# A two-layer hybrid encoder on one core: zero products ahead, halved first pages, norm rows in place, a held key rotation and another order at the end

## The chip, the cores and the metric

One core of one Trainium2 chip runs the whole program. The metric is the device time of one execution in microseconds (us); less is better. TensorE is called PE here, its weight load PEld, VectorE DVE, ScalarE ACT, GpSimd POOL, SyncE SP. Weights and activations lie in device memory (HBM); the working memory of the core is SBUF, and PE writes its sums to PSUM, of which one bank holds 128x512 numbers of 32 bits.

## The reference

x has 256 rows (tokens) of 4096 numbers. Two layers follow one another, then a last RMS norm:

```
h   = rmsnorm(x, norm_w)
a_q, a_k, a_v, a_g, r_q, r_k, r_v, r_g = split(h @ w_in)      # 4096 x 11264
att = silu(a_g) * attention(rope(rms(a_q)), rope(rms(a_k)), a_v)   # 16 heads, 4 for keys and values
ret = silu(r_g) * ret_norm * rms(retention both ways (r_q, r_k, r_v))  # 8 heads of 256
x   = x + concat(att, ret) @ w_out                            # 4096 x 4096
```

All is float32. `norm_w`, `ret_norm` and `final_norm` are gains by column.

## The kernel before

**Products.** The two projections are nearly all the work. The input projection has 11 blocks in each layer and the output projection 4; a block is two column tiles of 512 for all 256 tokens, so four quarters of 128 tokens by 512 columns. Its 4096 inputs are taken in 16 pairs of k tiles (two times 128 rows). In five pairs (`SEVEN`: 0, 3, 6, 9, 12) the 2x2 block product is made of seven products of sums, as Strassen does; the other eleven take eight, of which two are with the difference of the operands (`x3`). The sums go to seven PSUM banks, M1 to M7, and `combine` (L1266) adds these into the two results `ca` and `cb` when a bank has its last product. Each product is made of three matmuls, since an operand is split into a high part rounded to the matmul's type and a low rest: high by high, weight's low by operand's high, weight's high by operand's low (`product`, L822 to 826).

**Weight pages.** `Weights.load` (L385, DMA at L392 on SP's queue) brings 512 KB pages (`wraw`, five buffers). `parts` (L395) makes the high part `whi` on ACT and the low part `wlo` on DVE, in rings of five buffers, so a page's cast waits until PE has used the page five before it. A pair of `SEVEN` makes two more pages of sums on DVE (`wsum`). In five pairs of each block the second page is "far" (`far_parts`, L411): ACT writes `fhi` and its negative into `flo`, and a DMA of POOL's queue adds the page from HBM onto `flo` (L467), with one buffer each. Where the traces show L198, that is the helper through which every DVE and ACT operation is called.

**Operands.** `split_pair` (L499) turns rows of activations (`full`, 512 KB chunks of two pairs, eight to a stage) into operands: `x7h`, `x7l` for pairs of `SEVEN`; `x8h`, `x8l` and `x3` (`x` in the traces) for others. At a layer's input the gain `nw` is applied here: in place on ACT for pairs of `SEVEN`, and inside the cast and the subtraction for the others. Chunks come back from HBM through POOL's queue, but the last two of a stage are kept in SBUF (`put`, L611), turned by copies on ACT (`move`, L790), and split when `split_late` (L586) is called.

**Order.** The program writes one order for each engine and the engines keep it. A planner does that while it goes through the products: `now.t` counts PE's time by the costs of L43 to 60, a clock for DVE and one for ACT say when these would be done, and after each product `tick` (L744) lets waiting side work (attention, retention, splitting: lanes and tasks that `yield` a delay) go a step further when `Weights.room` (L469) finds that the next pages stay in time; there MARGIN is a reserve, PE_REST is the delay behind a side product, LANDING and FETCH are delays for DMAs, and AT_ONCE bounds the tasks begun. Where PE needs an operand that isn't there, `need` (L599) writes the missing steps at once.

**Places that the change touches.** `keys_values` (L1134) ends the block of keys and values: it loads tables (`plain_tables`, L315, the DMA of the gains at L321) and calls `rotary`, whose first DVE operations, C and S, multiply the tables by the gain. `retention_pair` (L1105) loads 256 KB of `ret_norm` gains on SP and multiplies the gate by them (`gate`, L893). `attention_rest` (L996) loads keys, values and queries (L1001, L787) and stores its result on POOL's queue (L1021). The last block's banks are closed in the order M2, M5, M3, M4 (`last_combine`, L1351); behind M3 and behind M4 `finish` (L1377) squares both tiles of one half of the tokens, sums ten columns of partial sums, takes the power on POOL (L346), and scales and stores eight tiles of 128x512 on SP's queue (L1401). At the start, SP brings the first chunk of x in two halves and the first pages; pair 1 is split first, by hand, then pair 0:

```python
first_rows(0)
weights.load()
...
split_operand(0, 0)
made(1)
begun()
...
begun()
made(0)
```

## Time and profile before

| | us |
|---|---|
| median of 3 runs | 2660.36 (2659.83 to 2660.64) |
| the profiled execution | 2660.69 |
| its span | 2658.5 |
| first matmul of PE starts | 8.95 |
| last matmul of PE starts | 2640.72 |
| mean granted PE clock | 0.993 |

A page of the profile tells for each engine the busy time, its share of the span and the number of instructions; the span is one execution on the chip. Groups of instructions have the line, the engine, the operation and "out<-in" by the program's names. In a timeline the first number is the start and the second the time it took, both in us, for `xN` instructions that follow one another; the bracket at the end tells how long the engine had been idle and what released it. Matmuls overlap: an instruction of 0.39 us may start 0.227 us after the one before. In a table of windows come the stretch, then the busy time and number of instructions of PE, PEld, DVE, ACT and POOL, then the clock granted to PE (1.00 is full), the busy share of the DMA engines and GB/s.

Three groups show how large the page work is:

```profile
L198 DVE TENSOR_TENSOR wlo<-wraw,whi 128x1024 fp32r<-128x1024 f32 (+1 forms) x812 | 894.9, 1120 | 281.4 <-ACT whi L198 275.4
L198 ACT CAST whi<-wraw 128x1024 fp32r<-128x1024 f32 (+1 forms) x812 | 778.8, 971 | 509.4 <-PE M L826 371.8
L467 POOL DMA_DIRECT2D flo<-in_w_in x108 | 97.4, 902 | 1076.1 <-ACT flo L198 1047.9
```

After the bar stand the busy time and the mean ns of one, then the idle time of the engine ahead of them and what ended most of it: ACT's casts wait for PE to free a ring buffer, DVE's low parts wait for the cast.

### The profile page before, as it was taken

The numbers are of one execution on the slowest core, as the hardware profiler recorded it, in microseconds if no ns is written. First come the engines' busy times: TensorE is split into PE (matmuls) and PEld (weight loads), VectorE is DVE, ScalarE is ACT, GpSimd is POOL, SyncE is SP. The second block draws the span as 40 slices with busy tenths as digits, with TensorE's granted clock in tenths as the row PEclk, the third lists the DMA queues.
The fourth block names the chain that finished last, engine by engine and source line by source line (L and its number), as shares of the span: only waits on it lengthen the run. The fifth ranks groups of instructions, "written<-read, shape, count | busy, mean of one in ns | idle before, by whom it ended". The sixth has DMA issues, their size and how long they took to land.

```text
span 2658.5 us, 33938 instructions
## 1 busy us (share of the span) xinstructions
PE 2609.4 (98%) x11742; PEld 2164.3 (81%) x11742; DVE 2153.8 (81%) x2701; ACT 1782.2 (67%) x2518; POOL 365.0 (14%) x508
## 2 busy tenths in 40 slices
PE   7999999999999999999999999999999999999997
PEld 5878888878888888888878888888888888888886
DVE  8878878878878899777989778877888788986775
ACT  6766776766665687665877666766666557876554
POOL 0011211211111010111111112211111111010000
PEclk9999999999999999999999999999999999999998
DMA  7888888888877887988988889889887788778895
GB/s 251 291 244 277 262 276 277 272 256 254 246 233 235 258 260 234 284 259 262 303 255 246 274 282 277 253 254 293 263 271 221 239 258 247 248 239 258 253 279 176
DMA packets 201981, 685.99 MB, mean 258 GB/s; under 512 B 24272, under 2 KB 30928, under 8 KB 201808
## 3 DMA queue, kind: packets, MB, share of 16 engines
q1 hardware_dynamic: 148912, 523.35, 56.4%
q0 software_dynamic: 52896, 160.46, 26.1%
q8 instruction: 92, 1.51, 0.2%
q14 instruction: 81, 0.66, 0.1%
HBM read 639.68 MB, written 44.04 MB: 257 GB/s over the span
## 4 chain that ended last, share of the span: by engine, by line
PE 81%; DVE 8%; DMA 6%; issue 2%; ACT 2%; POOL 1%; SPq 0%; DVEq 0%; POOLq 0%; ACTq 0%
PE M L825 26%; PE M L826 26%; PE M L824 26%; DVE wlo L198 4%; DMA flo<-in_w_in 2%; DMA wraw<-in_w_in 2%; DVE wsum L198 1%; PE ps L825 1%; PE ps L824 1%; PE ps L826 1%; DMA wraw<-in_w_out 1%; ACT whi L198 1%; DMA tables<-in_k_norm 1%; DVE ca L198 0%; DVE cb L198 0%
## 5 line engine op out<-in xcount | busy, mean ns | idle before, releaser
L198 DVE TENSOR_TENSOR wlo<-wraw,whi 128x1024 fp32r<-128x1024 f32 (+1 forms) x812 | 894.9, 1120 | 281.4 <-ACT whi L198 275.4
L198 ACT CAST whi<-wraw 128x1024 fp32r<-128x1024 f32 (+1 forms) x812 | 778.8, 971 | 509.4 <-PE M L826 371.8
L824 PE MATMUL M<-whi,x8h 128*128 128x512 f32 x1536 | 600.8, 391 | 0.5 <-DVE ca L198 0.5
L825 PE MATMUL M<-wlo,x8h 128*128 128x512 f32 x1536 | 600.4, 391 | 0.0
L826 PE MATMUL M<-whi,x8l 128*128 128x512 f32 x1536 | 600.0, 391 | 0.0
L824 PE MATMUL M<-whi,x7h 128*128 128x512 f32 x1050 | 410.0, 390 | 1.5 <-DVE cb L198 1.5
L825 PE MATMUL M<-wlo,x7h 128*128 128x512 f32 x1050 | 409.4, 390 | 1.9 <-DVE wlo L198 1.9
L826 PE MATMUL M<-whi,x7l 128*128 128x512 f32 x1050 | 409.0, 389 | 0.0
L198 DVE TENSOR_TENSOR wlo<-wsum,whi 128x1024 fp32r<-128x1024 f32 x300 | 365.5, 1218 | 24.1 <-ACT whi L198 23.5
L198 ACT CAST whi<-wsum 128x1024 fp32r<-128x1024 f32 x300 | 314.7, 1049 | 101.8 <-PE M L826 87.5
L824 PEld LDWEIGHTS M<-whi,x8h 128*128 128x128 f32 x1536 | 290.1, 189 | 60.8 <-DVE ca L198 0.9
L826 PEld LDWEIGHTS M<-whi,x8l 128*128 128x128 f32 x1536 | 289.9, 189 | 60.8
L825 PEld LDWEIGHTS M<-wlo,x8h 128*128 128x128 f32 x1536 | 290.1, 189 | 59.5
L198 ACT CAST fhi<-wraw 128x1024 fp32r<-128x1024 f32 x148 | 155.7, 1052 | 197.9 <-PE M L826 193.4
L467 POOL DMA_DIRECT2D flo<-in_w_in x108 | 97.4, 902 | 1076.1 <-ACT flo L198 1047.9
L824 PEld LDWEIGHTS M<-whi,x7h 128*128 128x128 f32 x1050 | 197.6, 188 | 43.7 <-DVE cb L198 2.9
L825 PEld LDWEIGHTS M<-wlo,x7h 128*128 128x128 f32 x1050 | 197.6, 188 | 42.3 <-DVE wlo L198 2.2
L826 PEld LDWEIGHTS M<-whi,x7l 128*128 128x128 f32 x1050 | 197.4, 188 | 41.3
L198 DVE TENSOR_TENSOR wsum<-wraw 128x1024 f32<-128x1024 f32 x150 | 182.6, 1218 | 45.0 <-DMA wraw<-in_w_in 39.8
L824 PE MATMUL M<-whi,x 128*128 128x512 f32 x512 | 199.9, 390 | 11.7 <-ACT whi L198 8.9
L825 PE MATMUL M<-wlo,x 128*128 128x512 f32 x512 | 200.4, 391 | 7.5 <-DVE wlo L198 7.5
L826 PE MATMUL M<-whi,x 128*128 128x512 f32 x512 | 200.2, 391 | 3.2 <-DVE x L198 3.2
(219 smaller groups left out, 3390.2 us busy)
## 6 DMA issues: line engine op xcount, KB each, us to landing
wraw<-in_w_in SPq DMA_DIRECT2D x703, 512.0 KB, 5.0
wraw<-in_w_out SPq DMA_DIRECT2D x256, 512.0 KB, 4.9
flo<-in_w_in POOLq DMA_DIRECT2D x108, 512.0 KB, 7.7
flo<-in_w_out POOLq DMA_DIRECT2D x40, 512.0 KB, 7.8
full<-next_dram POOLq DMA_DIRECT2D x18, 512.0 KB, 8.1
p_dram<-room POOLq DMA_DIRECT2D x64, 128.0 KB, 4.6
pT<-p_dram POOLq DMA_DIRECT2D x16, 512.0 KB, 9.8
next_dram<-room POOLq DMA_DIRECT2D x40, 128.0 KB, 5.5
```

The source lines that it names most:

```text
L198: return call(out, *args, **kwargs)
L467: self.adds.pop(0)[1]()
L824: nc.tensor.matmul(out, a[0], b[0], start=start, stop=False)
L825: nc.tensor.matmul(out, a[0], b[1], start=False, stop=False)
L826: nc.tensor.matmul(out, a[1], b[0], start=False, stop=stop)
```

## The change

- **Zeros first.** `warm` sets a small tile to zero and issues 36 matmuls of 128x256 on it (bfloat16, into a PSUM tile that nothing reads), ahead of everything else on PE.
- **First pages in halves.** The very first page is cast and subtracted in two halves of 128x512; the first block's first four products are sorted by half, with the `x3` product behind the other of its half; the first chunk's second half (pair 1) is loaded first, and pair 1's operand, and the first page, are written in an order by hand. The host gives x in plain columns of tokens, so operands of the first stage are cut out of `whole` rows.
- **Norm rows in place.** `ret_norm` joins the table `nw`, and its gains are applied to the rows of the output projection's operands (pairs 8 to 15) instead of the gate; the load of gains, the multiplication and a delay go from `retention_pair`. Gains are applied in place on ACT for all pairs but the very first, and what follows is the cast and subtraction without gains: where before `x8l` took four operations of 128x128 at a stage with gains, it takes one of 128x512 or two of 128x256.
- **Last block.** The order of the banks is M5, M2, M3, M4, and the last products of pair 14 on pages that are still in the ring (M4's) are moved to the end, behind M3's. Squares are taken by bank, one operation on 512 columns each, eight columns of partial sums; output tiles are scaled and stored in a list by hand with an engine named for each.
- **Key rotation.** `keys_values` yields LANDING between the tables' load and the rotation.
- **Planner numbers.** FETCH 14 to 12, FAR_LANDING 12 to 11, MARGIN 0.8 to 0, PE_REST 1.0 to 1.5, AT_ONCE 3 to 2. They enter the order of all side work.

In instructions (rows of the built programs, before to after): PE 11,744 to 11,816 with the loads of weights of the zeros, DVE 2425 to 2411, ACT 1720 to 1756, SP 102 to 82, POOL 282 to 281.

```diff
-STORE, FETCH = 8.0, 14.0
-FAR_LANDING = 12.0
-MARGIN = 0.8
+STORE, FETCH = 8.0, 12.0
+FAR_LANDING = 11.0
+MARGIN = 0.0
 EARLY = 0.7
 NEED = {"ak": 4, "ag": 3, "rk": 4, "rg": 4}
-PE_REST = 1.0
-AT_ONCE = 3
+PE_REST = 1.5
+AT_ONCE = 2
+WARM = 36
...
-FINAL_ORDER = ("M2", "M5", "M3", "M4")
+FINAL_ORDER = ("M5", "M2", "M3", "M4")
...
+        def taken(self):
+            while not self.raw:
+                self.later.pop(0)[1]()
+            return self.raw.pop(0)
...
+            for h in halves:
+                ac.copy(g.hi[:, h, :], src[:, h, :])
...
+                halves = (slice(0, 1), slice(1, 2)) if g is self.order[0] else (ALL,)
+                self.parts(g, self.taken(), halves, self.load)
...
+    def gains_of(p, stage):
+        layer, second = divmod(stage, 2)
+        if second and p < NP // 2:
+            return []
+        first = DEPTH * KT + layer * (KT // 2) + 2 * p - KT // 2 if second else layer * KT + 2 * p
+        return [nw[:, first + i : first + i + 1] for i in range(2)]
+    def split_pair(p, v, whole, stage):
+        gains = gains_of(p, stage)
+        now_first = stage == 0 and p == 1
...
-        if p in SEVEN and gains:
+        if gains and not now_first:
             for i in range(2):
-                u = v[:, :, i].rearrange("p m a t -> p (a m) t")
+                u = v[:, :, i].rearrange("p m a t -> p (a m) t") if whole is None else whole[:, i]
                 ac.activation(u, u, AF.Copy, scale=gains[i])
             yield
...
-            u = [w.rearrange("p i (m a t) -> p i m a t", m=MT, t=BLK) for w in (hi, lo)]
-            for i in range(2):
-                high(u[0][:, i], v[:, :, i], i)
-            yield
-            for i in range(2):
-                for m in range(MT) if gains else [ALL]:
-                    low(u[1][:, i, m], v[:, m, i], f32(u[0])[:, i, m], i)
-            ve.tensor_sub(x0, x0, x1)
-            yield
             g4 = [tokens(g[:, k]) for k in range(2)]
-            for i in range(2) if gains else [ALL]:
-                high(g4[0][:, i], x0[:, i], i)
-            yield
-            for i in range(2) if gains else [ALL]:
-                low(g4[1][:, i], x0[:, i], f32(g4[0])[:, i], i)
+            if now_first:
+                for i in range(2):
+                    ac.activation(hi[:, i], whole[:, i], AF.Copy, scale=gains[i])
+                yield
+                for i in range(2):
+                    ve.scalar_tensor_tensor(
+                        lo[:, i], whole[:, i], gains[i], f32(hi)[:, i], op0=ALU.mult, op1=ALU.subtract
+                    )
+                yield
+                ve.tensor_sub(x0, x0, x1)
+                for i in range(2):
+                    ac.activation(g4[0][:, i], x0[:, i], AF.Copy, scale=gains[i])
+                yield
+                for i in range(2):
+                    ve.scalar_tensor_tensor(
+                        g4[1][:, i], x0[:, i], gains[i], f32(g4[0])[:, i], op0=ALU.mult, op1=ALU.subtract
+                    )
+            else:
+                if whole is None:
+                    u = [w.rearrange("p i (m a t) -> p i m a t", m=MT, t=BLK) for w in (hi, lo)]
+                    pieces = [(u[0][:, i], u[1][:, i], v[:, :, i]) for i in range(2)]
+                else:
+                    pieces = [(hi, lo, whole)]
+                for h, _, src in pieces:
+                    ac.copy(h, src)
+                yield
+                for h, w, src in pieces:
+                    ve.tensor_sub(w, src, f32(h))
+                ve.tensor_sub(x0, x0, x1)
+                yield
+                ac.copy(g4[0], x0)
+                yield
+                ve.tensor_sub(g4[1], x0, f32(g4[0]))
...
-        if gain is not None:
-            ve.tensor_mul(acc, acc, gain.unsqueeze(1).to_broadcast([P, MT, NB]))
-            drop()
...
-        gain = page([P, NB], "gain")
-        nc.sync.dma_start(gain, ret_norm[L.index, i * NB : (i + 1) * NB].partition_broadcast(P))
-        yield LANDING / 2
-        yield from gate(gacc, L, gain)
+        yield from gate(gacc, L)
...
         L.plain = plain_tables(L.index)
+        yield LANDING
         yield from rotary(kacc, L, "ak", k_dram)
...
+        if first_order:
+            flat[:4] = sorted(flat[:4], key=lambda v: (v[4], v[2][1] == 2))
+        used = list(dict.fromkeys((v[1], v[3]) for v in flat if not is_far(None, v[1], v[3])))[-RING:]
+        def at_end(v):
+            return v[1] == NP - 1 or (last and v[0] == order[-1] and v[1] == NP - 2 and (v[1], v[3]) in used)
+        end = [v for v in flat if at_end(v)]
         end.sort(key=lambda v: order.index(v[0]))
-        flat[-len(end) :] = end
+        flat = [v for v in flat if not at_end(v)] + end
...
+        room = []
+        def square(m, c, i):
+            n = N_OUT - 2 + i
+            outs[n] = c[i]
+            if not room:
+                room.append(t(pm, [P, NB], "ps"))
+            ac.activation(room[0], c[i][:, m, :], AF.Square, accum_out=sums[:, m, n : n + 1])
         def last(bank, acc, c):
             if bank == "M1":
...
                 ve.tensor_add(ca[:, 1, :], ca[:, 1, :], res[0, 1])
                 ve.tensor_add(cb[:, 0, :], cb[:, 0, :], res[1, 0])
                 ve.tensor_add(ca[:, 0, :], ca[:, 0, :], res[0, 0])
+            elif bank == "M2":
+                combine(bank, acc, c)
+                square(0, c, 0)
             elif bank == "M5":
+                ve.tensor_add(cb[:, 0, :], cb[:, 0, :], acc["M5"])
                 ve.tensor_add(cb[:, 1, :], cb[:, 1, :], acc["M5"])
-                ve.tensor_add(cb[:, 0, :], cb[:, 0, :], acc["M5"])
-            elif bank in ("M2", "M3", "M4"):
+                square(1, c, 1)
+            elif bank == "M3":
                 combine(bank, acc, c)
-            if bank == "M3":
-                finish(0, c)
+                square(0, c, 1)
+                r[0] = last_rstd(0)
+                for n in (0, 2):
+                    finish(0, n, ac)
             elif bank == "M4":
-                finish(1, c)
-        return last
-    def finish(m, c):
-        for i in range(2):
-            n = N_OUT - 2 + i
-            outs[n] = c[i]
-            for k in range(2):
-                at_sum = n + 2 * k
-                ac.activation(
-                    junk,
-                    c[i][:, m, k * RV : (k + 1) * RV],
-                    AF.Square,
-                    accum_out=sums[:, m, at_sum : at_sum + 1],
-                )
-        r = t(sp, [P, 1], "last", 2)
-        ve.tensor_reduce(r, sums[:, m, :], axis=AX.X, op=ALU.add)
-        rsqrt(r, r, 1, D_MODEL)
-        for n in range(N_OUT):
+                combine(bank, acc, c)
+                square(1, c, 0)
+                finish(0, 7, ve)
+                r[1] = last_rstd(1)
+                for n, e in ((1, ve), (6, ve), (3, ve), (4, ac), (5, ve)):
+                    finish(0, n, e)
+                for n, e in ((0, ac), (1, ve), (2, ac), (3, ve), (5, ve), (4, ac), (6, ve), (7, ve)):
+                    finish(1, n, e)
+        r = {}
+        def finish(m, n, engine):
             v = outs[n][:, m, :]
             if n >= N_OUT - 2:
-                ve.scalar_tensor_tensor(v, v, r, fn[n - N_OUT + 2], op0=ALU.mult, op1=ALU.mult)
-            elif n % 2:
-                ve.tensor_scalar_mul(v, v, r)
+                ve.scalar_tensor_tensor(v, v, r[m], fn[n - N_OUT + 2], op0=ALU.mult, op1=ALU.mult)
+            elif engine is ve:
+                ve.tensor_scalar_mul(v, v, r[m])
             else:
-                ac.activation(v, v, AF.Copy, scale=r)
+                ac.activation(v, v, AF.Copy, scale=r[m])
             nc.sync.dma_start(out[m * P : (m + 1) * P, columns(n)], v)
+        return last
+    def last_rstd(m):
+        r = t(sp, [P, 1], "last", 2)
+        ve.tensor_reduce(r, sums[:, m, :N_OUT], axis=AX.X, op=ALU.add)
+        rsqrt(r, r, 1, D_MODEL)
+        return r
...
-        for k in range(0, KG * SEQ, step):
+        for k in reversed(range(0, KG * SEQ, step)):
             nc.sync.dma_start(full[c][:, k : k + step], xT[c, :, k : k + step])
+    def warm():
+        ps = t(pm, [P, NB], "ps")
+        ve.memset(junk, 0.0)
+        for _ in range(WARM):
+            nc.tensor.matmul(ps[:, :RV], junk[:, :P], junk, start=True, stop=True)
...
+    warm()
     first_rows(0)
     weights.load()
     turn = Turn(0, first_rows)
     turn.fetched, turn.cut, turn.freed, turn.at[2] = 3, 2, NP, 1.3 * LANDING
     turning.append(turn)
     split_operand(0, 0)
+    for _ in range(2):
+        waiting[1].step()
+    begun()
     made(1)
-    begun()
...
-        "norm_wT": np.ascontiguousarray(a["norm_w"].reshape(DEPTH * KT, P).T),
+        "norm_wT": np.concatenate([a["norm_w"].reshape(-1, P), a["ret_norm"].reshape(-1, P)]).T,
```

More of the change, by code (lines that the diff above doesn't have):

```diff
@@ L393, in load, with parts @@
                 self.raw.append(r)
-        def parts(self, g, src, halves=ALL, then=None):
+        def taken(self):
+            while not self.raw:
+                self.later.pop(0)[1]()
+            return self.raw.pop(0)
+        def parts(self, g, src, halves=(ALL,), then=None):
             g.hi = t(wp, [P, 2, NB], "whi", RING, F32R)
             g.lo = t(wp, [P, 2, NB], "wlo", RING, F32R)
-            ac.copy(g.hi[:, halves, :], src[:, halves, :])
+            for h in halves:
+                ac.copy(g.hi[:, h, :], src[:, h, :])
             g.high_at = ac.until + PASS
@@ L403, in low @@
                 ve.after(g.high_at)
-                ve.tensor_sub(g.lo[:, halves, :], src[:, halves, :], f32(g.hi)[:, halves, :])
+                for h in halves:
+                    ve.tensor_sub(g.lo[:, h, :], src[:, h, :], f32(g.hi)[:, h, :])
                 g.low_at = ve.until + PASS
@@ L441, in begin @@
             elif g.kind == PAGE_B:
-                self.parts(g, self.b, slice(1, 2), then=self.load)
+                self.parts(g, self.b, (slice(1, 2),), self.load)
             else:
@@ L609, in need, with put @@
                 advance()
[L611 removed]
+    def put(c, v, stage):
         if c >= NCH - 2:
@@ L615, in put @@
             own(-1)
-            late.append((c, l))
+            late.append((c, stage))
         else:
@@ L891, in rotary, with gate @@
         return rs if kind == "aq" else None
-    def gate(acc, L, gain=None):
+    def gate(acc, L):
         e = page([P, MT, NB], "tanh")
@@ L1022, in attention_rest @@
         drop(2)
-        put(g, sgT)
+        put(g, sgT, 2 * L.index + 1)
     def retention_weights(L, i):
@@ L1411, in first_sums @@
         load_small()
-        part = t(sp, [P, MT, N_OUT + 2], "sums", 2)
+        part = t(sp, [P, MT, N_OUT], "sums", 2)
         loaded = []
@@ L1483, in hybrid_encoder @@
         last_layer = l == DEPTH - 1
-        sums = t(sp, [P, MT, N_OUT + 2], "sums", 2)
+        sums = t(sp, [P, MT, N_OUT], "sums", 2)
         outs = {}
```

57 lines of the change are left out of this document (20 added, 37 removed).

## The prediction

> **What bounds the kernel now.** I read the page's head first, then what TensorE (PE) waited for, then the timeline at each wait.
>
> ```profile
> span 2658.5 us, 33938 instructions
> PE 2609.4 (98%) x11742; PEld 2164.3 (81%) x11742; DVE 2153.8 (81%) x2701; ACT 1782.2 (67%) x2518; POOL 365.0 (14%) x508
> ```
> PE is the bound. Its starts lie 0.227 us apart for 11,070 matmuls of 128x512 and 0.120 us for 672 of 128x256: 2512.8 + 80.6 = 2593.4 us. The other 65 us are all that a change of order can touch: 8.95 before the first matmul, 17.8 after the last one's start (2640.72), and 38.5 in which starts lay further apart, of those 17.5 before 50 us, 8.8 at 150, 4.7 at 500 to 600, 0.7 at 625, 3.0 at 1250 to 1350, 4.2 in smaller places. The waits of PE (total, times, longest):
>
> ```profile
> PE M L825 <- DVE wlo L198: 9.4, 5, 5.8
> PE M L824 <- ACT whi L198: 8.9, 1, 8.9
> PE M L825 <- DMA flo<-in_w_in: 5.5, 6, 2.2
> PE M L826 <- DVE x L198: 3.2, 1, 3.2
> ```
> A wait costs more than itself: after the 5.79 us one at 150 the starts lie 0.427 apart from 156.74 to 162.51, which is 5.8 x (1 - 0.227/0.427) = 2.7 more.
>
> The profiled execution took 2660.69: span 2658.5 and 2.2 around it. It stands 0.33 above the median shown; I sum against it.
>
> **Key rotation held: -8.8.** Timeline of SP, DVE and PE there:
>
> ```profile
> 146.04 0.42 SPq L321 DMA_DIRECT2D tables<-in_k_norm  x1
> ...
> 154.51 0.29 DVE L198 TENSOR_TENSOR C<-tables 128x128 f32<-128x128 f32 x1 [8.76 <-DMA tables<-in_k_norm]
> ...
> 155.47 1.22 DVE L198 TENSOR_TENSOR wlo<-wraw,whi 128x1024 fp32r<-128x1024 f32 x1
> ...
> 156.74 0.80 PE L825 MATMUL M<-wlo,x 128*128 128x512 f32 x1 [5.79 <-DVE wlo L198]
> ```
> DVE stands 8.76 us on the tables, the page's low part behind them is late, PE stands 5.79 and is slow after it. In the built order the C and S multiplies now come some 7 us of PE time later, behind other pages' low parts. The tables take 8.4 us from issue to landing, so DVE may still stand 1 to 2 us; the next low part behind them has about 2 us in hand and DVE little before it. I take the whole 8.8 as gone; were the cover gone, up to 8 would stay. Layer 2 has the same hold; there PE lost nothing before.
>
> **Norm rows in place: +8.2 at the start of layer 2.** Sixteen gain loads, sixteen DVE multiplies of 128x1024 and split subtractions go; 36 ACT instructions come. DVE and ACT have room (81 and 67%), so busy time is worth nothing; place is. At layer 2's first block the last chunk's pairs (14 and 15) are split from `cb`:
>
> ```profile
> 1405.81 1.06 ACT L198 ACTIVATE flo<-fhi 128x1024 fp32r<-128x1024 f32 x1
> 1406.77 1.69 ACT L198 ACTIVATE x8h<-cb,nw 128x256 fp32r<-128x256 f32 x4
> 1408.37 0.56 ACT L198 COPY ca<-M 128x512 f32<-128x512 f32 x1
> ```
> Before, these four stood 6.6 us of PE time ahead of the product that reads them. In the built order they come last of all, when that product is due: behind two page casts whose buffers PE frees only 0.9 us before the due time, then four in-place scalings, then four casts, then DVE's subtractions. With casts of 1.05, scalings at 0.41 apart and casts of 0.40, counted from the due time: page casts end at +1.5, scalings at +3.15, x8h at +4.65, DVE's first low part at +5.2; the x3 pieces cost 0.45 more. PE stands 5.65, and its slow stretch costs 2.6 as at 150. Ends: 0 if ACT gets ahead (the page casts released sooner), 11 if pair 15 stands as well. I take 8.2, nearest to the rows. The same scalings everywhere else come early enough; they move sums at the block boundaries of 1339 and 1343 earlier (-0.7) and leave bank releases tighter at three others (+0.7).
>
> **Planner numbers: -4.5 on the far pages.** A far page's low part is a DMA onto `flo`; POOL issues it.
>
> ```profile
> 535.26 0.55 POOL L1021 DMA_DIRECT2D next_dram<-sgT  x1 [13.12 <-DVE sgT L198]
> 535.80 0.56 POOL L1001 DMA_DIRECT2D kv<-kv_dram  x1
> 536.31 0.57 POOL L787 DMA_DIRECT2D q<-q_dram  x1
> 538.08 0.88 POOL L467 DMA_DIRECT2D flo<-in_w_in  x1 [1.19 <-ACT flo L198]
> ...
> 550.98 0.50 PE L825 MATMUL M<-flo,x8h 128*128 128x512 f32 x1 [2.24 <-DMA flo<-in_w_in]
> ```
> This one landed 12.9 us after issue because two 512 KB loads went out just ahead of it. It cost 4.9 with the slow stretch. The others: 515 0.44, 625 0.65, 1469 1.5, 1715 0.8, 1822 1.25, two of 0.1; all: 9.8. They arise where POOL has four stores (0.55 us each) that wait for a DVE transpose ahead of the page's issue. The new constants shuffle all side work; in the built order the places of before are clear, one such group remains (about 563 us of PE time), and four places have loads close by (1252, 1785, 911, 2208). I leave 5.3 standing; ends 1 and 20.
>
> **Zeros first and halved pages: -0.9.** Windows of the start (PE, PEld, DVE, ACT, POOL busy; clock; DMA share; GB/s):
>
> ```profile
> 0.00:20.00 20.00, 10.48 (x31) 7.74 (x31) 11.67 (x26) 11.38 (x21) 0.21 (x4) 1.00 0.72 264
> 20.00:40.00 20.00, 13.13 (x46) 9.53 (x46) 19.35 (x36) 17.07 (x30) 1.02 (x1) 0.91 0.73 253
> ...
> 25.63 0.51 PE L825 MATMUL M<-wlo,x7h 128*128 128x512 f32 x1 [1.86 <-DVE wlo L198]
> ...
> 41.47 0.79 PE L826 MATMUL M<-whi,x 128*128 128x512 f32 x1 [3.18 <-DVE x L198]
> ```
> To 41.5 us DVE is the bound (19.35 of 20). The first real product moves from 8.95 to about 7.5 (half a page's cast 0.56 instead of 1.05; the row of x it needs lands at 4.36, before at 5.12). The 36 matmuls of zeros (0.12 to 0.21 each, 4.3 to 7.7 us) end by then or a little after. But PE waits again for DVE's low parts at 20.54 and 25.63 and x at 41.47, and the built order gives those 20.55, 25.65 and about 40.6: pair 4's x8l is one subtraction of about 0.7 instead of four of together 1.13. So the early start is given back, 0.9 stays. The sixteen slow steps from 8.95 to 15.85 that a warm PE would spare are 3.0 us: below 20 us of DVE's chain, they too are hidden. Ends -3.9 and +2 (zeros that run slowly and hold the first product to 8.5 or later).
>
> The Trainium skill (TensorE: Matmul & The Clock Gate, "Part 1: The HAM clock gate") has the array slow until about 3.4 us of sustained work. By it the zeros, which are such work, make the first products fast, and if they were on the path the sum would be 3.0 lower. The trace agrees on the spacing: its clock changes lie multiples of 3.413 us apart. It differs on the drop: a 1.86 us gap (23.77 to 25.63) was enough.
>
> **Tail: -2.6.** Last products in another order, one square per bank, an output tile scaled and stored by itself:
>
> ```profile
> 2645.25 0.68 DVE L198 TENSOR_TENSOR ca<-ca,M 128x512 f32<-128x512 f32 x1
> ...
> 2648.18 0.16 DVE L198 TENSOR_REDUCE last<-sums 128x1 f32<-128x10 f32 x1 [2.26 <-ACT junk L198]
> ...
> 2654.34 0.47 SPq L1401 DMA_DIRECT2D out<-cb  x1
> ```
> From T = 2640.72 before: the last bank's add waits behind five operations to T+4.5, the scaling ends at T+11.1, the last store issues at T+13.6 and lands at T+16.55, end T+17.76. After: nine matmuls of M4 (2.0 us) stand behind M3's last one, beside them M3's add (0.69), its square (0.7, by two halves of 0.42 now) and the factor (reduce 0.16 to first scaling, 1.1 to 1.2): known at about T+0.9, first store issued T+1.65, landing 2.15 later, then sixteen stores of 256 KB at most 0.67 apart (the pitch before): last lands 1.65 + 2.15 + 15 x 0.67 = T+13.85, end T+15.1. The second row's factor follows at about T+3.3 and scaling ends at T+7.65, ahead of the stores. Ends -3.4 and -1.
>
> **Sum:** -8.8 + 8.2 - 0.7 + 0.7 - 4.5 - 0.9 - 2.6 = -8.6: 2652.1, stated as 2652. 0.2% of 2660 is 5.3, about what a measurement of this kernel can tell from no change: faster is under 2655.0, slower over 2665.7.
>
> **Rivals.**
> - No stall at layer 2's start: ACT has time between the page casts, and `tick` may find room. For it: the four are ready long before. Against: the order puts the casts first and PE frees their buffers last. 2643.9.
> - Far pages as bad as now: 4.5 more, 2656.6. For it: the cause is POOL's order, which the change shuffles rather than mends.
> - Slower: each of the four places named at POOL goes like the one at 548, 4 x 4.9 = 19.6 in place of 5.3: 2666.4. It decides from four such places on; their loads are out 2 us or more ahead of the page's issue, which speaks against.
> - Tables still late, DVE's wait moved to the next low part: 8.8 more, 2660.9. Against: the 2 us in hand.
> - Warm start worth all 3.0: 2649.1. Against: DVE's busy share to 41 us.
>
> **How the numbers follow.** Forecast (2648 to 2656) 0.44, of which 0.04 lies above 2655; no stall 0.14; far pages as now 0.18; POOL's places 0.10; tables late 0.08; warm start 0.06. Faster 0.40 + 0.14 + 0.06 = 0.60; within 0.04 + 0.18 + 0.08 = 0.30; slower 0.10. The range 2643 to 2662 leaves out the slower rival and the tails of the others.
>
> **What would show it.** Right: no wait on tables near 150; one wait of PE of about 5 us on x8l or ACT near 1412, the largest after 50 us; waits on flo of about 3 us together; last store 13 to 14 us after the last matmul; DVE's low parts at 20.5 and 25.6 as before. Wrong: PE without a wait from 8 to 30 us, new waits on flo of 2 us or more, or none at 1412.

## The result, and the profile after

The changed kernel takes 2680.24 us, median of 4 runs (2678.84 to 2685.05), beside 2660.5 (2659.83 to 2667.82) of the kernel before: a ratio of 1.0071, 95% interval 1.005 to 1.0093. It is 0.7% slower, by 18.2 us from one profiled execution (2660.69) to the other (2678.84). The head of the page and the waits of PE (total, times, longest) of the changed kernel; L851 to 853 are the three matmuls that were L824 to 826, L200 is the helper that was L198:

```profile
span 2676.8 us, 33938 instructions
PE 2620.1 (98%) x11778; PEld 2169.8 (81%) x11778; DVE 2134.8 (80%) x2620; ACT 1799.5 (67%) x2554; POOL 366.2 (14%) x508
```

```profile
PE M L852 <- DMA flo<-in_w_in: 12.4, 6, 6.5
PE M L851 <- ACT x L200: 10.8, 3, 5.5
PE M L851 <- DVE cb L200: 6.8, 3, 3.3
PE M L852 <- DVE wlo L200: 4.8, 7, 1.7
PE M L852 <- DMA flo<-in_w_out: 2.4, 1, 2.4
```

DVE is less busy than before (2134.8 us against 2153.8) and the waits for low parts have halved (4.8 against 9.4), as the change means. But the waits on flo went from 5.5 to 14.8 us, those on `cb` from 1.5 to 6.8, and those on ACT's `x` from 2.7 (at 34 us) to 10.8, of which 5.5 stand at 34 us and 5.0 at 1413.

Both programs run the same matmuls in nearly the same order, so the start of the k-th matmul (the zeros not counted) can be set side by side. How far the changed kernel is behind, from the two traces (below, a wait is placed where it begins, and a place or a slice of the span "loses" what the starts of matmuls there lie further apart than the prediction's 0.227 and 0.120 us):

| matmul | before, us | changed behind by | what lies in the stretch |
|---|---|---|---|
| 100 | 49.17 | -0.57 | the start |
| 500 | 140.13 | +0.66 | flo at 101, `cb` at 111 |
| 800 | 217.75 | -5.38 | held rotation; flo at 155 |
| 1700 | 413.28 | -1.48 | flo at 227, 243 and 317 |
| 4100 | 941.30 | -7.63 | the waits on flo of before at 515, 548, 625 are gone |
| 4700 | 1072.51 | -1.04 | start of the first output projection |
| 5900 | 1347.62 | +1.23 | flo at 1297 |
| 6200 | 1415.88 | +8.64 | start of layer 2 |
| 8000 | 1813.76 | +5.28 | waits on flo of before gone |
| 8600 | 1943.70 | +14.10 | flo at 1846 |
| 10100 | 2272.42 | +14.10 | nothing |
| 10700 | 2404.76 | +20.31 | start of the second output projection |
| last | 2640.72 | +20.31 | nothing |
| end | 2658.48 | +18.36 | tail |

The worst flo, by the timeline of ACT, POOL and PE in the changed kernel:

```profile
1834.63 1.06 ACT L200 ACTIVATE flo<-fhi 128x1024 fp32r<-128x1024 f32 x1
...
1835.58 0.57 POOL L1045 DMA_DIRECT2D next_dram<-sgT  x1 [8.82 <-DVE sgT L200]
1836.14 0.56 POOL L1025 DMA_DIRECT2D kv<-kv_dram  x1
1836.68 0.55 POOL L814 DMA_DIRECT2D q<-q_dram  x1
1837.20 0.94 POOL L476 DMA_DIRECT2D flo<-in_w_in  x1
...
1853.11 0.80 PE L852 MATMUL M<-flo,x8h 128*128 128x512 f32 x1 [6.46 <-DMA flo<-in_w_in]
```

ACT was done at 1835.69; POOL stood at a store that waited for DVE, issued it and two loads of 512 KB, and then flo, which landed 15.9 us after its issue (at 1853.07), where the median of these transfers is 7.8. With the slow stretch behind it the place costs 9.0.

The start of the output projection, DVE and PE:

```profile
983.59 1.23 DVE L200 TENSOR_TENSOR wsum<-wraw 128x1024 f32<-128x1024 f32 x1 [4.07 <-DMA wraw<-in_w_out]
...
997.21 0.80 PE L851 MATMUL M<-whi,x7h 128*128 128x512 f32 x1 [3.30 <-DVE cb L200]
```

Two pages of 512 KB were issued at 973.41 and 973.83, just behind a flo at 973.36, and landed 8.5 and 9.7 us later; DVE stood 4.07 at the first operation on them, everything behind it was late, the last of it the sums that free a bank. Before, the same two pages were issued at 980.53 and 982.41, ahead of the flo (983.77), landed in 4.3 and 5.1, and PE waited for nothing.

### The profile page after: what moved, and what is told of

Same layout as the page of the kernel before. It is cut to its first block, busy times and chain, and to the rows that moved or that the text cites. A ratio compares the mean times of both kernels' runs of the same rounds, so it can differ in the third digit from the quotient of the medians.

```text
span 2676.8 us, 33938 instructions
## 1 busy us (share of the span) xinstructions
PE 2620.1 (98%) x11778; PEld 2169.8 (81%) x11778; DVE 2134.8 (80%) x2620; ACT 1799.5 (67%) x2554; POOL 366.2 (14%) x508
## 4 chain that ended last, share of the span: by engine, by line
PE 82%; DVE 8%; DMA 6%; ACT 2%; issue 2%; POOL 1%; SPq 0%; DVEq 0%; ACTq 0%; POOLq 0%
PE M L852 26%; PE M L853 26%; PE M L851 26%; DVE wlo L200 4%; DMA wraw<-in_w_in 3%; DMA flo<-in_w_in 2%; DVE wsum L200 1%; PE ps L852 1%; PE ps L853 1%; PE ps L851 1%; DMA wraw<-in_w_out 1%; ACT whi L200 1%; DVE cb L200 0%; DVE ca L200 0%; DMA flo<-in_w_out 0%
## 5 line engine op out<-in xcount | busy, mean ns | idle before, releaser
L200 DVE TENSOR_TENSOR wlo<-wraw,whi 128x1024 fp32r<-128x1024 f32 (+1 forms) x813 | 895.5, 1119 | 305.3 <-ACT whi L200 300.4
L200 ACT CAST whi<-wraw 128x1024 fp32r<-128x1024 f32 (+1 forms) x813 | 779.7, 969 | 509.0 <-PE M L853 365.6
L851 PE MATMUL M<-whi,x8h 128*128 128x512 f32 x1536 | 600.8, 391 | 1.1 <-ACT whi L200 0.6
L851 PE MATMUL M<-whi,x7h 128*128 128x512 f32 x1050 | 410.1, 391 | 6.8 <-DVE cb L200 6.8
L200 DVE TENSOR_TENSOR wlo<-wsum,whi 128x1024 fp32r<-128x1024 f32 x300 | 365.3, 1218 | 25.9 <-ACT whi L200 25.7
L200 ACT CAST whi<-wsum 128x1024 fp32r<-128x1024 f32 x300 | 314.8, 1049 | 97.8 <-PE M L853 92.5
L851 PEld LDWEIGHTS M<-whi,x8h 128*128 128x128 f32 x1536 | 289.9, 189 | 61.8 <-ACT whi L200 1.7
L200 ACT CAST fhi<-wraw 128x1024 fp32r<-128x1024 f32 x148 | 155.7, 1052 | 199.2 <-PE M L853 191.8
L851 PEld LDWEIGHTS M<-whi,x7h 128*128 128x128 f32 x1050 | 197.6, 188 | 49.3 <-DVE cb L200 8.4
L200 DVE TENSOR_TENSOR wsum<-wraw 128x1024 f32<-128x1024 f32 x150 | 182.8, 1219 | 48.2 <-DMA wraw<-in_w_in 37.1
L851 PE MATMUL M<-whi,x 128*128 128x512 f32 x512 | 200.9, 392 | 11.8 <-ACT x L200 10.8
```

Source lines behind the costliest of these rows:

```text
L200: return call(out, *args, **kwargs)
L851: nc.tensor.matmul(out, a[0], b[0], start=start, stop=False)
```

## The experiments

The kernel before was run again beside each group of runs and took 2659.7 to 2662.1 us in the median, so a difference of 2 us between runs of different groups tells nothing. At a single place, too, two executions of the same order differ by up to 2 us: the two traces of "flo first in the changed kernel" and of "gains in the cast" have the same order on every engine to 1266 us, and their distance moves by 1.9 us near 155.

"flo first" below is one edit, by which no engine but POOL gets another order; the traces show PE, DVE, ACT and SP in the same order with and without it. `weights.add(True)` issues the transfers onto flo that are due; the replacement shown is made at all of POOL's transfers but flo's own.

```diff
     weights = Weights()
+    def pool_dma(*args, **kwargs):
+        weights.add(True); nc.gpsimd.dma_start(*args, **kwargs)
...
-        nc.gpsimd.dma_start(v, src)
+        pool_dma(v, src)
```

**The changed kernel with the numbers of before.**

```diff
-STORE, FETCH = 8.0, 12.0
-FAR_LANDING = 11.0
-MARGIN = 0.0
-PE_REST = 1.5
-AT_ONCE = 2
+STORE, FETCH = 8.0, 14.0
+FAR_LANDING = 12.0
+MARGIN = 0.8
+PE_REST = 1.0
+AT_ONCE = 3
```

> The changed kernel with the five planner numbers of the kernel before (FETCH 14, FAR_LANDING 12, MARGIN 0.8, PE_REST 1.0, AT_ONCE 3). Theory: the new waits of PE on flo (14.8 us, about 19 with their slow stretches) and on cb behind late weight pages near 993 and 2317 (about 11) come from where the new numbers put POOL's and SP's transfers; then this gives 2650 to 2662, and such waits sum to under 12 us. Rival: they come from the norm rows scaled in place, which stay here; then it stays at 2672 to 2684 with waits on cb of 3 us near the same two places. Under both, the 5 us wait near 1413 stays.

2675.05. Waits on flo sum to 16.5 us, more than in the changed kernel, so for flo the theory fell: with the old numbers it is as late, partly at other places (153, 546, 622, 1318, 1724, 1866). The losses at the starts of the output projections fell from 12.8 to 3.6, with waits on `cb` of 0.7 us each, so here the theory holds and the rival falls, although the time lies in the rival's range.

**The kernel before with the new numbers.** The same lines the other way round.

> The kernel before with the five new planner numbers alone. Theory (the numbers place the transfers badly): 2670 to 2684, PE's waits on flo over 12 us, the wait behind the tables near 150 still there. Rival (the rows in place cost it): 2655 to 2663, waits on flo at most as before (5.5 us).

2692.49, even above the range: 14.5 us of waits on flo, and waits on `wlo`, `cb` and `x7l` near 994 to 1062 and 2317 to 2383. The wait behind the tables is there. In these two and in the changed kernel flo is late by 14.5 to 16.5 us: three new orders, with the new numbers and with the old. The order of before was the one with few such places.

**flo first in the changed kernel.**

> The changed kernel, in which a far page's transfer onto flo that is already due is issued on POOL's queue ahead of any other transfer of POOL; all other engines keep their order. Theory: flo is late since POOL issues it 1.3 to 2.8 us after ACT is done and behind loads and stores that land first; then the four waits (3.3 near 155, 1.1 near 243, 2.4 near 1297, 6.5 near 1846) fall to under 1 each, 12 to 17 us in all with the slow stretches: 2663 to 2668. Rival: all transfers share the same engines, and flo lands as late whatever stands ahead in the queue: 2676 to 2682, with the four waits over half of now.

2666.19, 14 us less. The same place as above, by POOL's timeline, ACT being done with flo at 1829.55 (L501 is now the line of all its other transfers):

```profile
1829.85 0.93 POOL L476 DMA_DIRECT2D flo<-in_w_in  x1 [9.45 <-ACT flo L200]
1830.44 0.89 POOL L501 DMA_DIRECT2D next_dram<-sgT  x1
1831.00 0.87 POOL L501 DMA_DIRECT2D kv<-kv_dram  x1
1831.52 0.88 POOL L501 DMA_DIRECT2D q<-q_dram  x1
```

The store and the loads are the same and now stand behind; PE waits there for nothing. Of the waits on flo one is left, 3.1 us near 155, where the edit can't help, since the stores ahead (L1159 of the changed kernel) are written before the page is begun. Theory confirmed at three places of four.

**The scalings written early at layer 2's start.**

```diff
         while starts and late:
-            split_late()
+            split_late(); [v.step() for v in waiting[-2:]]
```

> The changed kernel, in which the four in-place scalings of the last chunk at the start of layer 2 are written when the chunk is handed on, not when PE needs its operands; little else moves. Theory: PE's 5 us wait near 1413 comes from the scalings and casts behind two page casts; it falls to 2 us or less, 4 to 7 us less in all: 2673 to 2676. Rival: PE would wait there as long for DVE's low parts behind the same pages: 2679 to 2682, with a wait of 4 us or more on x8l or wlo near 1413.

2681.65: the rival was right in the time and in kind, though not in size (it had 4 us or more). ACT's wait fell to 2.9, and PE then waited 3.0 for DVE's `x`, which stood behind the pages' low parts; the place lost 9.5 us instead of 7.6. (The profiled execution, 2686.56, was the slowest of four, and lost more at other places too, where nothing was changed: 4.5 at 247.) ACT's queue was the first of two late ones.

**flo first in the kernel before.**

> The kernel before, in which a due transfer onto flo is issued ahead of POOL's other transfers; the order of the other engines is that of before. Theory (POOL's order makes flo late): its waits on flo, 5.5 us and 9.8 with the slow stretches, fall under 1.5, so 2649 to 2655 beside 2660.5 of before. Rival: the order of before was already as good as it gets and a flo moved up delays the loads and stores behind it: 2658 to 2665.

2652.45, 0.9961 of before (0.9947 to 0.9976). Waits on flo fall from 5.5 to 1.4 us, and flo first is all that differs. Confirmed.

**Gains of layer 2's input in the cast, on top of flo first.**

```diff
+        as_before = stage == 2 and p not in SEVEN
-        if gains and not now_first:
+        if gains and not now_first and not as_before:
...
+            elif as_before:
+                u = [w.rearrange("p i (m a t) -> p i m a t", m=MT, t=BLK) for w in (hi, lo)]
+                for i in range(2):
+                    ac.activation(u[0][:, i], v[:, :, i], AF.Copy, scale=gains[i])
...
```

> The changed kernel with flo's transfers first (as the run before it of that name, 2666.2), and with the gains of layer 2's input for the pairs of eight products applied as before, in the cast and in the subtraction, not in place. Theory: the scalings in place fill ACT at the start of layer 2 and push the last two pairs to the time when PE needs them; without them the 5.0 us wait on x near 1407 goes, 7 to 8 us with its slow stretch: 2657 to 2660. Rival: the wait is due to the planner's numbers, and stays: 2664 to 2668.

2665.52, no better. The wait on `x` fell from 5.0 to 1.1 and the loss at that place from 8.0 to 1.3, as the theory says; but the slice 1300 to 1350 lost 5.6 instead of 1.4, with 1.9 us on `cb` at 1338. There the first chunks are split, and DVE has four subtractions of 128x128 for a pair instead of two of 128x256 ahead of the sums. So scaling in place gives DVE before the stage about 4 of the 6.7 us that it takes from ACT at its start. The rest of what was gained went in the scatter named above, near 155 and 229, ahead of anything that this edit changes.

**No zeros, with flo first.**

```diff
-    warm()
     first_rows(0)
```

> The changed kernel with flo's transfers first, without the 36 products of zeros. Theory: DVE is the bound at the start, so matmul 100 begins within 0.7 us of where it does with the zeros and the time stays at 2665 to 2668. Rival: the warm clock is worth its 3.0 us: 2668.5 to 2670, with matmul 100 some 3 us later.

2668.91, by the time in the rival's range. But matmul 100 starts at 48.63 without and at 49.56 with zeros, and in all nine traces that have the zeros at 47.30 to 49.56: a gain of 3 us is excluded, one of less than 1 is not, and the mechanism is the theory's. The difference of 2.8 us in the ends of the two spans arises after 930 us, in waits on `wlo` at 985 and 1277 behind transfers; the runs of the two overlap (2665.48 to 2673.53, and 2663.71 to 2670.2).

**Old numbers too.** The gains in the cast, flo first and the five old numbers.

> The changed kernel with flo's transfers first, layer 2's input gains in the cast, and the five planner numbers of before: what is left of the change is the start, the held rotation, the norm rows folded into the output projection, the order at the end. Theory: the new numbers crowd DVE at the end of the input projections (waits on cb near 991 and 2305, 5.2 us each); with the old ones these shrink to under 2 each: 2644 to 2654, below both kernels. Rival: the rows in place bring these waits: 2655 to 2660.

2660.66: above both ranges, 4.9 less than with the new numbers. The starts of the output projections lost 2.0 and 1.8 instead of 5.8 and 4.9, so this part of the theory holds. What kept the time up stood near 153: 8.1 us on flo, 10.5 with the slow stretch.

**The held rotation alone, on the kernel before with flo first.**

```diff
         L.plain = plain_tables(L.index)
+        yield LANDING
```

> The kernel before with flo's transfers first (2652.5) and the key rotation held, nothing else of the change. By the prediction's step, 8.8 us go: 2643 to 2645, and PE has no wait near 150. Rival: what is late next is the far page's flo, which landed at 154.46 before, under the cover of the wait for the tables: PE then waits 3 us on flo near 154, 4 to 5 with the slow stretch, and 2647 to 2650 results. Second rival: the C and S operations stand only 2.5 us of PE time behind the tables' issue in this order and DVE still waits on them: 2650 to 2654.

2650.78, 1.7 less than without; the runs of the two overlap (2650.24 to 2651.24, and 2648.98 to 2653.86). PE's wait of 5.4 near 150 is gone. DVE still stood 2.91 us on the tables, as the second rival said, PE did not feel it there, but waited 2.3 for `cb` at 197, and 0.5 at 111. Matched by matmuls, the held rotation gains 8.1 us up to 165 and gives 5.2 of them back by 215.

**The low stores later too.**

```diff
         for i in range(2):
+            if i: yield 4.0
             for k in range(MT):
```

> As the held rotation alone, and the stores of the values' low parts come 4 us later in the planner's time than those of the high parts, which puts the C and S operations some 6 us of PE time behind the tables' issue. Theory (the tables' transfer is the rest of the wait): 2643 to 2648, no wait on tables of over 2 us on DVE near 150. Rival: flo's landing decides there, 2647 to 2650, with 3 us or more of PE on flo near 154.

2649.82, above the theory's range, and not told from the run before it (2647.11 to 2651.25). DVE no longer waits on the tables; matmul 600 starts 7.9 us and matmul 800 5.9 us earlier than in the kernel with flo first alone, so at the place the hold is worth what the theory says. Later waits on flo (2.2 at 1303, 1.3 at 1490, 1.1 at 2407) took a part of it back.

**What gained, together.** The changed kernel with flo first, the low stores later, the old numbers, and the norm rows as before: of the change remain start, hold and tail.

> The changed kernel with flo's transfers first, the planner numbers of before, the gains of layer 2 in the cast and the gains of the retention in the gate, as before, and the low stores later: what stays of the change is the start, the held rotation and the order at the end. Theory: each is worth what the two traces show by itself (0.6 to 1.5 at the start, 4 to 8 at the rotation, 2 at the end), on top of the 2652.5 of the kernel before with flo first: 2640 to 2647. Rival: the reshuffled order brings new waits of that size: 2650 to 2656.

2645.37 (2645.05 to 2646.25), 0.9942 of before (0.9926 to 0.9959): in the theory's range, 0.6% below the kernel before. Against the trace of the kernel before with flo first it is 8.2 us shorter: 0.2 at the start, 7.8 at the rotation, 2.0 behind the last matmul, less 1.7 lost in between. Its head:

```profile
span 2643.8 us, 33973 instructions
PE 2610.2 (99%) x11778; PEld 2165.6 (82%) x11778; DVE 2150.3 (81%) x2661; ACT 1782.3 (67%) x2511; POOL 364.1 (14%) x508
```

PE has as much to do as before, in 14.7 us less.

**The new numbers on the kernel before with flo first.**

> The kernel before with flo's transfers first and the five new planner numbers. Theory: the numbers cost by themselves, apart from flo's order: DVE and ACT are crowded where blocks meet (waits on cb and x7l near 1006, 1060, 1355, 2328 and 2382 in the run of the numbers alone, about 17 us with slow stretches): 2666 to 2674. Rival: with flo first the numbers cost nothing: 2650 to 2656.

2675.20, 22.7 above that base: the theory's mechanism (2.6 on `cb` at 996, 1.3 on `x7l` at 1050, the same in layer 2), and a little more than its range. Waits on flo are 1.3. So the numbers cost apart from flo's order. Beside the same numbers without flo first (2692.49) this is 17 us less: a third pair in which flo first pays.

**One number at a time**, each on the kernel before with flo first (2652.45). AT_ONCE was not run alone.

```diff
-FAR_LANDING = 12.0
+FAR_LANDING = 11.0
```

> The kernel before with flo's transfers first (2652.5), and FAR_LANDING 11 for 12 alone. Theory: of the five numbers, which together cost 22.7 us here, this one moves side work to where blocks meet, since only with it the built order has ACT and DVE crowded near 1010 and 2307 us of PE time, as with all five: 2664 to 2674. Rival: the cost is spread over the numbers: 2655 to 2660.

2677.68.

```diff
-MARGIN = 0.8
+MARGIN = 0.0
```

> The same base with MARGIN 0 for 0.8 alone. Theory (FAR_LANDING carries the cost): 2650 to 2656. Rival (the missing reserve lets side work in too late): 2660 or more, with waits on wlo and cb.

2654.49.

```diff
-PE_REST = 1.0
+PE_REST = 1.5
```

> The same base with PE_REST 1.5 for 1.0 alone. Theory (FAR_LANDING carries the cost): 2650 to 2656. Rival (later steps behind PE crowd the ends of blocks): 2658 or more.

2656.51, at the edge between the two.

```diff
-STORE, FETCH = 8.0, 14.0
+STORE, FETCH = 8.0, 12.0
```

> The same base with FETCH 12 for 14 alone. Theory (FAR_LANDING carries the cost): 2650 to 2656. Rival (attention's operands are split before they have landed, and ACT or DVE stands): 2658 or more.

2680.92: the theory, that one number carries all, fell. FETCH alone costs 28 and FAR_LANDING alone 25, and all five together 23, so the costs don't add up. The missing reserve (MARGIN), which I would have blamed, costs 2, and PE_REST 4; the four runs are of another group than their base, so each cost is uncertain by some 2 us. FAR_LANDING's lies at the starts of the output projections, as the theory said (7.6 us from 936 to 1075, 6.2 from 2284 to 2422), and of layer 2 (8.9 from 1302 to 1430). How FETCH costs is seen in PE's waits and DVE's timeline of that run:

```profile
PE ps L826 <- DVE aql L198: 11.2, 6, 1.9
```

```profile
342.29 0.69 DVE L198 TENSOR_TENSOR wlo<-wraw,whi 128x512 fp32r<-128x512 f32 x1 [4.48 <-ACT whi L198]
342.90 1.28 DVE L198 TENSOR_TENSOR aql<-q,aqh 128x512 fp32r<-128x512 f32 x2
```

The queries' low parts stand in DVE's queue behind a page's low part, which waits for ACT's cast, which waits for PE to free a buffer; six times PE comes to the attention's product first. These six places lose 24 of the 31 us by which the trace is longer.

**The rows in place again**, in the kernel of 2645.37.

> The kernel that keeps what gained (2645.4), with the norm rows scaled in place again, all of them, as in the changed kernel. Theory: the rows in place cost by themselves at the start of layer 2 (8 to 9 us near 1400) and 1 to 2 us at the start of each output projection, and give back up to 4 before layer 2's start, since DVE has less to do there: 2650 to 2659. Rival: with the old planner numbers the rows cost nothing that counts: 2643 to 2648.

2658.62, 13 more. Matched by matmuls the two traces differ by +3.2 at the start of the first output projection, -2.4 before 1347, +9.3 at layer 2's start, +1.8 at the second output projection: the theory's places and prices. At layer 2's start PE waits 1.1 for ACT's `x` and 4.4 for DVE's.

**Two numbers back in the changed kernel**, with flo first.

```diff
-STORE, FETCH = 8.0, 12.0
-FAR_LANDING = 11.0
+STORE, FETCH = 8.0, 14.0
+FAR_LANDING = 12.0
```

> The changed kernel with flo's transfers first (2666.2), and of the five numbers the two back at their old values that cost 25 and 28 us by themselves on the kernel before (FETCH 14, FAR_LANDING 12). Theory (these two numbers are bad by themselves): 2650 to 2661. Rival: a number is good or bad only with the others and with the order it meets; the built order here crowds DVE at the start of both output projections (near 1033 and 2330 us of PE time), and 2664 to 2685 results, with waits on x near there.

2691.69, 25.5 more than 2666.19: the rival. The same two values that cost 25 and 28 us by leaving the old order cost 25.5 together by coming back into the new one, with 4.4 us waits on `x` at 1078 and 2406. Neither value of the two is good by itself.

## Why the prediction was wrong, step by step

It gave 2652.1 from 2660.69 (-8.6); the profiled execution came to +18.2. Two steps failed, the one on the far pages and the +0.7 for bank releases. The others held within a microsecond, each at its place, if the new wait on flo at 155 is counted with the far pages. Of its signs of being wrong one came, new waits on flo of 2 us or more (14.8 us in all, where it had about 3); of its signs of being right came the wait of about 5 us near 1412, though not as the largest, and PE's wait behind the tables was gone.

- **Key rotation, -8.8: held**, for the wait behind the tables; DVE still stands 0.80 us on them. The place as a whole gained 5.3: the slice 150 to 200 went from 8.8 to 3.5 lost, and what is left is a wait of 3.29 on flo, which landed late before too (154.46) under the cover of the longer wait. By the timeline of POOL and PE:

```profile
146.30 1.49 POOL L1159 DMA_DIRECT2D kv_dram<-vl  x2 [3.59 <-DVE vl L200]
147.77 0.95 POOL L476 DMA_DIRECT2D flo<-in_w_in  x1
...
158.98 0.50 PE L852 MATMUL M<-flo,x8h 128*128 128x512 f32 x1 [3.29 <-DMA flo<-in_w_in]
```

  POOL's stores wait 3.59 for DVE, with flo behind them, which ACT had ready at 144.93. The step asked what is late next among the low parts only, and not in POOL's queue.

- **Layer 2's start, +8.2: held**, 7.6 measured. ACT's queue ran as worked out, by the timeline of ACT and PE:

```profile
1413.19 1.99 ACT L200 CAST whi<-wraw 128x1024 fp32r<-128x1024 f32 x2 [1.55 <-PE M L853]
1415.10 1.70 ACT L200 ACTIVATE cb<-cb,nw 128x256 f32<-128x256 f32 x4
1416.70 1.31 ACT L200 CAST x8h<-cb 128x256 fp32r<-128x256 f32 x4
...
1418.83 0.80 PE L851 MATMUL M<-whi,x 128*128 128x512 f32 x1 [4.99 <-ACT x L200]
```

Two casts that wait for PE's buffer, four scalings, four casts: a wait of 4.99, forecast as 5.65 (5.2 to DVE's first low part, 0.45 for the pieces of x3). With the gains in the cast it falls to 1.1, so the rows in place cause it here. They are not its only cause: with FAR_LANDING 11 alone, on the kernel before, PE waits 5.35 for ACT's `x` at 1418 without them. That mending ACT alone doesn't help was not in the step; DVE's queue is as late.

- **Planner numbers, -4.5 on the far pages: failed.** They lose 20.8 us instead of 9.8: 0.9 at 101, 3.5 at 155, 2.3 at 227 and 243, 0.9 at 317 and 600, 4.2 at 1297, 9.0 at 1846, slow stretches included. Two of the four places that the slower rival named are among them (1252 and 1785 us of PE time, 1297 and 1846 on the clock); 911 and 2208 cost nothing, 155 and 243 were not named. That its price, 19.6, comes near 20.8 is luck: the two of its places that counted cost 13.2, and the other 7.6 came at places that it did not name. The places of before are clear, as the step said; what failed is that it took this for a gain, where each of the three new orders of POOL's queue that were run brought places of its own. The numbers are not needed for it: with the old ones in the changed kernel the waits on flo are 16.5 us. That POOL's order is the cause is shown by flo first, in three pairs (14, 9 and 17 us). Why each number moves side work to just these places was not followed through the planner.
- **"Bank releases tighter at three others", +0.7: failed**, with 12.8 us lost at the starts of the output projections. The step looked at how far ahead of PE the sums stand in the order, and not at the weight pages in DVE's queue ahead of them, which were late. With the old numbers 3.6 are left, so most of it comes with the numbers; the new numbers alone bring this on the kernel before also. flo first doesn't help: with it the two starts lose 5.2 and 5.3. That the transfer onto flo beside them is what made the pages late is argued from the issue and landing times, not shown by a run of its own. Other runs fit it: issued 1.7 and 1.3 us ahead of the flo (the changed kernel with the numbers of before), the two pages land in 5.3 and 6.7 and that start loses 1.9; 0.9 and 0.5 us ahead (the new numbers on the kernel before with flo first), 6.2 and 7.7, and it loses 4.9. This loss was in none of the rivals.
- **Start, -0.9: held in size** (-0.57 at matmul 100 in this pair; -1.1 from the mean of the ten traces with the old start, 49.23, to that of the nine with the new one and the zeros, 48.15). Not held is what the step said of the waits: none stands at 25.6 in this trace, and the longest is 5.46 on ACT's `x`, from 34.8 to 40.3. The step called DVE the bound to 41.5 us and left out the wait of 2.75 on ACT's `x` that the trace of before has there (to 37.55). At matmul 80 the pair is 0.5 behind; its gain by matmul 100 comes from a slow stretch that ends at 44.8 instead of 46.5, which no step forecast: luck, as far as the runs show. The rival of the warm clock fell: without zeros matmul 100 starts at 48.63, among those with them.
- **Tail, -2.6: held in kind**, -1.95. The first store was issued 1.7 us after the last matmul's start, as forecast, the last one 11.1 after it, against 13.6 before; the end came at +15.8, forecast 15.1. The pitch was a little better than forecast: SP issued the sixteen over 9.4 us (forecast 10.05), with gaps where it waited for a tile (2665.08 to 2665.41, 2670.64 to 2671.06). The term that was off is the landing: the last store took 3.52 us, and the step had carried the first one's 2.15 to the last, although the last of before took 2.93.
- **The sum.** 26.8 us lie between forecast and measurement: 15.5 of flo (20.8 - 9.8 + 4.5) and 12.1 at the output projections make 27.6; the small terms take the rest back.

## What to carry to other kernels

When a planner's constants change, read the order of every queue anew, the DMA queues first: for each transfer that the bound engine waits for, what is issued ahead of it and what that waits for; a rule that such a transfer goes first (two lines here, and a call at each other transfer of the queue) gained 14, 9 and 17 us in the three pairs where it was run. Price a constant only on the order it will meet: here two new values cost 25 and 28 us, each alone in the old order, and taking both out of the new order cost 25.5. A wait that is taken away can uncover the next late thing at the same place (flo at 155, DVE's `x` behind ACT's), and an engine with a third of its time free, as ACT here, still makes PE wait if its queue stands in the wrong order.

## What the runs showed of the hardware

- A transfer of 512 KB onto flo (input projection, changed kernel) landed 7.8 us after issue in the median, and 15.9 behind a store and two loads of 512 KB. Moved ahead of these it landed in 7.6, and PE did not wait. Stores ahead of it tell less: of all 148, the 17 with two or more stores and nothing else in the 3 us before landed in 8.8 in the median (at most 11.2), the 101 with nothing ahead on POOL's queue for 9 us in 7.0 (at most 11.3). The Trainium skill (DMA: Bandwidth & Descriptors, "Queues, rings and completion order") has each DMA engine take turns between the queues that have work for it; that descriptors are consumed in ring order it says there of SP's and ACT's queues. On POOL's queue the trace shows the order of issue at this place: store, two loads and flo landed at 1844.27, 1846.81, 1849.32 and 1853.07 in the changed kernel, and flo first, at 1837.50, ahead of the others at 1839.55, 1841.48 and 1844.05, when it was issued first.
- PE's granted clock halved after most of the longer waits, for one or more stretches of 3.41 us: 997.1 to 1000.5 after 3.30 us of waiting, 1416.9 to 1423.8 after 4.99, 1850.4 to 1857.3 after 6.46. In these places a 3.3 us wait cost about 5, a 5 us wait near 8. Waits of 2.39 us (1297), 1.86 us (before, at 23) and, with the new numbers on the kernel before, 1.30 us (1060) halved it too, one of 3.29 (155) and one of 1.12 (243) in the changed kernel did not, so the length of the wait alone doesn't tell. The Trainium skill (TensorE: Matmul & The Clock Gate, "Part 1: The HAM clock gate") has the clock fall after at least one idle window of about 3.4 us; all four of the waits up to 3.30 us that halved it are shorter than that, so here the measurement decides.
- With the zeros the clock was full at 3.83 us and the first products ran at 0.23 us; without them it was full at 11.4 us and they ran at 0.43 to there. With the zeros it was lost again at 20.9 us and without them at 18.2, after waits of PE for DVE (1.68 us in both), and matmul 100 did not start later without zeros.
